# Decoder trunk on one core: TensorE's instructions chained in the order of emission

## The chip, the core and the metric

The kernel runs on one NeuronCore of one Trainium2 chip. A core has TensorE (PE; its weight loads are listed apart, as PEld), VectorE (DVE), ScalarE (ACT), GpSimd (POOL) and SyncE (SP, which issues the DMAs here). Each engine takes its own list of instructions in the order in which that list was written when the kernel was compiled, and waits on semaphores for what other engines must have done. The metric is the device time of one launch in microseconds. The kernel before takes 2995.44 us, the median of 3 runs (2991.24 to 2997.36).

## The reference

Two layers over 2048 prompt tokens and 8 sample tokens. Each layer projects the normed input, sends the columns through three mixers (mLSTM, Mamba-2 SSD, sliding-window attention), and projects back:

```python
def _layer(x, pos, conv_buf, ssm_h, C0, n0, m0, kc, vc, norm_w, w_in, ..., w_out):
    u = _rmsnorm(x, norm_w) @ w_in                      # 1024 -> 4880
    (aq, ak, av, ao, az, ai, af, bz, bxbc, bdt, cq, ck, cv, cz) = _split(u, IN_SIZES)
    ha, C1, n1, m1 = _mlstm(aq, ak, av, ai + a_ib, af + a_fb, C0, n0, m0)
    ya = _rmsnorm(ha, a_nw) * sigmoid(ao) * silu(az)
    xbc, conv1 = _causal_conv(bxbc, conv_buf, conv_w, conv_b)
    bx, bB, bC = _split(xbc, (B_WIDTH, B_GROUPS * B_STATE, B_GROUPS * B_STATE))
    yb, h1 = _ssd(bx, softplus(bdt + dt_bias), -exp(A_log), bB, bC, ssm_h)
    yb = _rmsnorm((yb + D_skip * bx) * silu(bz), b_nw)
    q, k = _rope(_rmsnorm(cq, qn_w), pos), _rope(_rmsnorm(ck, kn_w), pos)
    yc = _swa(q, k, cv, kc, vc, sinks) * silu(cz)       # window 128, softmax with sinks
    return x + concatenate([ya, yb, yc]) @ w_out, states   # 1536 -> 1024
```

Everything is float32; the states and the windows of keys and values are outputs too.

## The kernel before

**Tiling.** The prompt goes in blocks of 512 tokens: 4 blocks a layer, 8 in all. A block's input projection is done by groups of columns (`g0`, `qk`, `v`, `o`, `z`, `x0`, `x1`, `cq`, `cz`, `bz`), each of 8 chunks of 128 input features. The output projection of a block is two halves of 12 chunks, and it is put between groups `z` and `x0` of the next block. That makes 832 chunks.

**A chunk** (`multiply`, L500 to L542) is 12 matmuls, here called products: 4 banks (tokens or columns by 128) times 3 parts, because each float32 factor is cut into a high and a low part and three of the four part products are kept. In the first and the last chunk of a group all three parts of bank 0 come first, then those of bank 1, and so on. In the chunks between, the two products that need the high weight part come first for all four banks, then the third. L519 and L521 are the two forms of a product (weights moving or standing). In the first block of a layer, and in the output projection of its third, each chunk ends with two more matmuls for the sample tokens (L541, L542).

**PSUM.** A group accumulates in four banks (`pj`), which is all that the pool `pj` has, so the next group's bank t can only be written when the last group's bank t has been read out (evacuated). For `z`, `cz` and `bz` the read-out is a SiLU: a tanh on ACT (L561), then a product on DVE that reads the bank again (L562). The other groups are copied out by ACT, and the output projection by one DVE addition (L1291). The other four banks (`mx`) turn over among all the small work.

**The mixers** are Python generators, one step from `yield` to `yield`: mLSTM (`mix_a`, L837 to L873), SSD (`mix_b`, L951 to L995), attention (`pre_c`, `main_c`, L1108 to L1212), and more for gates, convolution, norms and sample tokens. In a chunk that isn't the last of its group, `pump` is called after every third product; at the end of every chunk it is called once. It goes through the streams in a fixed order and emits at most one step of each, when the stream's rate allows it and when a small model of the engines (`Clock`) holds the last step of the stream for finished and a bank for free. So in the emitted order, mixer work stands only after a multiple of three products: all PE instructions of a step are emitted in one piece.

**What sets the order.** The program is traced inside `tile.TileContext(nc, schedule_with_timeline_sim=True)`. At its end, the framework makes each engine's list: it plays the traced instructions through its own timing model and gives an engine, at each time of that model, the earliest emitted instruction that the model holds for ready. So the list of an engine can differ from the order of emission, and once made it is fixed. A few DMAs are pinned with `tc.keep_in_program_order`. The diff touches the end of `run` (L1832 to L1905).

Of the kernel before, what the change touches and what calls it, by code (L numbers as in the profile page):

```python
# [184 lines left out]
class Build:  # L185
# [1662 lines left out]
    def run(self):  # L1848
        nc = self.nc
        self.L = {0: self.layer_params(0)}  # L1850
        chunks = self.plan()
        PD, PS = 4, 2
        pre = self.dec_prep(0, None)
        self.con = con = self.consts()
        for i in range(PD):
            self.xraw(i)
            self.load_chunk(chunks[i])
            if i == 0:
                next(pre)
                next(con)  # L1860
        for i in range(PD, KD):
            self.xraw(i)
        for h in range(2):
            self.tokens(0, h, (12, 0)[h])
        for i in range(PS):
            self.xparts(i, self.L[0])
            self.split_chunk(chunks[i])
            self.flush()
        for _ in pre:
            pass  # L1870
        for i in range(PS, KD):
            self.xparts(i, self.L[0])
        grp = None
        for i, ch in enumerate(chunks):
            S = ch['S']
            if ch['pos'] == 0:
                self.before(ch)
                grp = self.banks(ch['dec'])
                if ch['g'] == 'out' and 'y' not in ch:
                    self.prep_y(ch)  # L1880
                    self.flush()
            if i + PD < len(chunks):
                self.load_chunk(chunks[i + PD])
            if i + PS < len(chunks):
                self.split_chunk(chunks[i + PS])
            if i + 1 < len(chunks) and chunks[i + 1]['g'] == 'out':
                nx = chunks[i + 1]
                self.drain(*({4: 'be', 0: 'a', 8: 'c'} if nx['S']['last'] else {0: 'c', 4: 'e'}).get(nx['k'], ''))
                self.prep_y(nx)
            if ch['g'] == 'out' and not S['last'] and ch['pos'] == (8 if ch['half'] == 0 else 5):  # L1890
                self.load_res(ch)
            if ch['g'] == 'out' and S['last'] and ('res', ch['half']) not in S and ch['k'] == (5 if ch['half'] else 0):
                self.load_res(ch)
            if ch['pos'] == ch['nk'] - 1:
                self.drain(*{'v': 'b', 'o': 'a', 'cq': 'ad', 'bz': 'v', 'x0': 'vs', 'x1': 'vs'}.get(ch['g'], ''))
            self.multiply(ch, grp)
            if ch['pos'] == ch['nk'] - 1:
                if ch['g'] == 'out':
                    self.evac_out_end(ch, grp[1])
                else:  # L1900
                    self.evac_end(ch['S'], ch['g'], grp[1])
            self.pump(ch['w'], BACKE if ch['pos'] >= ch['nk'] - EDGE else BACKO if ch['g'] == 'out' else BACK)
            self.lates()
            self.after(ch)
        self.flush()  # L1905


def build(nc):
# [27 lines left out]
```

## Time and profile before

| what | value |
| --- | --- |
| median of 3 runs | 2995.44 us |
| the profiled execution | 2994.12 us |
| its span, first to last instruction | 2992.3 us |
| PE busy | 2903.5 us, 97% |
| DVE, ACT, POOL busy | 1912.3, 1235.0, 920.3 us |
| DMA | 187 GB/s over the span |

A line of the timeline gives the start in us from the span's start, the length in us, engine, line of the kernel, operation, tile written and tiles read, shape, and how many like it follow without another of that engine between; in square brackets stands how long the engine had been idle before and what ended that. The length of a matmul is modelled and overlaps the next one, so the pace of PE is read from starts. A line of the waits gives the waiting engine with its tile and line, the releaser, the us in total, the number of waits and the longest. A line of the windows gives the stretch, its length, busy time and (x) count of PE, PEld, DVE, ACT and POOL, the granted TensorE clock (1.00 is 2.4 GHz, 0.50 is 1.2 GHz), the DMA share and GB/s.

### The profile page before, as it was taken

Reading aid. Unit: us, or ns where it says so; the run is one execution under the profiler, and the core shown is the slowest. Engines: PE = TensorE matmul, PEld = TensorE weight load, DVE = VectorE, ACT = ScalarE, POOL = GpSimd, SP = SyncE. Lnnn points to the kernel's source line nnn. Section 1 sums busy time; section 2 is a strip of 40 time slices with the busy share of each in tenths; the row PEclk is TensorE's granted clock in tenths of the full one; section 3 lists DMA queues with packets and bytes.
Section 4 is the critical chain, followed back from the end, with each engine's and each line's share of the span. In section 5 each row is a group of like instructions: output and inputs, shape, how many; then the busy total and the mean of one; then the engine's idle time right before and its main releaser. Section 6 shows DMA issues by size and latency. Waiting matters only on the chain.

```text
span 2992.3 us, 42253 instructions
## 1 busy us (share of the span) xinstructions
PE 2903.5 (97%) x14454; PEld 2373.4 (79%) x14454; DVE 1912.3 (64%) x4323; ACT 1235.0 (41%) x3219; POOL 920.3 (31%) x968
## 2 busy tenths in 40 slices
PE   8999999999999999999999999999999999999988
PEld 7787877788878888888788778887887778788876
DVE  6378567778476763477644686477755677645774
ACT  5343555235432453325544345432444225532344
POOL 5336325244131430116422552332421132200321
PEclk9999999999999999999999999999999999999999
DMA  8755558754575434655556745687545754355533
GB/s 279 241 197 168 174 184 284 248 170 141 164 247 189 151 117 143 199 171 182 184 187 215 240 159 183 205 274 232 161 156 177 244 174 160 131 163 165 177 112 124
DMA packets 245995, 558.82 MB, mean 187 GB/s; under 512 B 49308, under 2 KB 82236, under 8 KB 245732
## 3 DMA queue, kind: packets, MB, share of 16 engines
q1 hardware_dynamic: 245780, 556.12, 57.6%
q8 instruction: 114, 1.87, 0.3%
q14 instruction: 101, 0.83, 0.1%
HBM read 430.46 MB, written 127.87 MB: 187 GB/s over the span
## 4 chain that ended last, share of the span: by engine, by line
PE 71%; DVE 13%; DMA 8%; POOL 3%; ACT 2%; issue 2%; SPq 1%; POOLq 0%; DVEq 0%; ACTq 0%
PE pj L519 29%; PE pj L521 27%; DMA wr<-in_w_in 2%; PE mx L1203 2%; PE mx L1152 2%; PE mx L984 1%; DMA unit<-bcd 1%; DVE quad L659 1%; PE mx L542 1%; PE mx L541 1%; POOL hl L498 1%; ACT unit L1173 1%; PE mx L993 1%; PE mx L1252 1%; DMA unit<-us 1%
## 5 line engine op out<-in xcount | busy, mean ns | idle before, releaser
L521 PE MATMUL pj<-hl,xTh 128*128 128x512 f32 (+1 forms) x3072 | 945.4, 383 | 17.2 <-ACT hl L494 7.6
L519 PE MATMUL pj<-xTh,hl 128*128 128x512 f32 x2240 | 727.5, 402 | 4.8 <-ACT xTh L1259 2.9
L521 PEld LDWEIGHTS pj<-hl,xTh 128*128 128x128 f32 x3072 | 564.6, 189 | 129.0 <-DVE quad L562 8.3
L521 PE MATMUL pj<-hl,xTl 128*128 128x512 f32 (+1 forms) x1536 | 580.4, 381 | 0.0
L519 PE MATMUL pj<-parts,hl 128*128 128x512 f32 x2016 | 518.9, 404 | 15.1 <-DVE parts L1266 8.3
L519 PEld LDWEIGHTS pj<-xTh,hl 128*128 128x128 f32 x2240 | 421.5, 190 | 100.9 <-ACT xTh L1259 3.9
L519 PEld LDWEIGHTS pj<-parts,hl 128*128 128x128 f32 x2016 | 366.9, 189 | 96.1 <-DVE parts L1266 11.2
L519 PE MATMUL pj<-xTl,hl 128*128 128x512 f32 x1120 | 436.0, 398 | 1.9 <-DVE xTl L1266 1.9
L498 POOL TENSOR_TENSOR hl<-wr,hl 128x512 fp32r<-128x512 f32 (+1 forms) x232 | 318.9, 1380 | 356.3 <-ACT hl L494 311.2
L521 PEld LDWEIGHTS pj<-hl,xTl 128*128 128x128 f32 x1536 | 291.1, 189 | 52.5
L1195 POOL TENSOR_TENSOR parts<-parts,cst 128x512 fp32r<-128x512 f32 x120 | 158.6, 1339 | 409.0 <-ACT parts L1188 392.3
L519 PEld LDWEIGHTS pj<-xTl,hl 128*128 128x128 f32 x1120 | 211.2, 189 | 47.7 <-DVE xTl L1266 2.3
L1266 DVE SCALAR_TENSOR_TENSOR parts<-quad,lp,parts 128x512 fp32r<-128x512 f32 x168 | 143.0, 852 | 155.4 <-ACT quad L1263 62.4
L494 ACT ACTIVATE hl<-wr 128x512 fp32r<-128x512 f32 (+1 forms) x232 | 142.2, 615 | 234.2 <-PE mx L542 49.6
L1032 POOL TENSOR_TENSOR unit<-quad,rpqn 128x256 f32<-128x256 f32 x32 | 24.3, 759 | 441.6 <-PE mx L951 166.8
L1173 ACT ACTIVATE unit<-unit,c_m,c_sc 128x128 f32<-128x128 f32 x256 | 123.3, 483 | 69.3 <-DVE c_m L1164 68.8
L1259 ACT ACTIVATE parts<-quad,lp 128x512 fp32r<-128x512 f32 x112 | 80.4, 720 | 155.9 <-PE pj L519 141.1
L659 DVE SCALAR_TENSOR_TENSOR quad<-quad,lp,quad 128x512 f32<-128x512 f32 x192 | 141.8, 781 | 0.3
L1189 DVE TENSOR_TENSOR parts<-mx,parts 128x512 fp32r<-128x512 f32 x64 | 44.0, 687 | 90.2 <-ACT parts L1188 81.0
L384 POOL TENSOR_TENSOR quad<-quad 128x512 f32<-128x512 f32 x24 | 33.5, 1398 | 217.1 <-ACT quad L382 216.4
L1181 ACT ACTIVATE unit<-unit,c_m 128x128 f32<-128x128 f32 x256 | 81.3, 392 | 19.4 <-DVE c_m L1179 19.2
L541 PE MATMUL mx<-hl,samS 128*66 128x512 f32 (+1 forms) x208 | 83.4, 403 | 0.9 <-ACT hl L494 0.9
(409 smaller groups left out, 4551.3 us busy)
## 6 DMA issues: line engine op xcount, KB each, us to landing
hl<-kept SPq DMA_DIRECT2D x552, 512.0 KB
kept<-hl SPq DMA_DIRECT2D x184, 512.0 KB
wr<-in_w_in SPq DMA_DIRECT2D x168, 256.0 KB
hl<-kept SPq DMA_DIRECT2D x48, 272.0 KB
quad<-in_xT SPq DMA_DIRECT2D x40, 256.0 KB
quad<-in_x_prompt SPq DMA_DIRECT2D x16, 512.0 KB
wr<-in_w_out SPq DMA_DIRECT2D x32, 256.0 KB
x<-quad SPq DMA_DIRECT2D x32, 256.0 KB
```

The costliest lines, as they stand in the source:

```text
L494: nc.scalar.activation(h, r, AF.Copy)
L498: nc.gpsimd.tensor_tensor(lw, r, h.bitcast(F32), op=ALU.subtract)
L519: nc.tensor.matmul(ps[t], w[:, tt], a, start=st and first, stop=en and last)
L521: nc.tensor.matmul(ps[t][:, :N], a[:, tt], w[:, :N], start=st and first, stop=en and last)
L541: nc.tensor.matmul(pd[:66, :N], self.samS[:, k, :], hi[:, :N], start=st, stop=False)
L659: nc.vector.scalar_tensor_tensor(acc, u[:, j:j + 512], cw[:, j, c:c + 1], acc, op0=ALU.mult, op1=ALU.add)
L1152: nc.tensor.matmul(o, q, kz[:, a, s, 0:nk, :].rearrange("p n c -> p (n c)"), start=s == 0, stop=s == 1)
L1173: nc.scalar.activation(P(a, j), P(a, j), AF.Exp, bias=nm[:, j:j + 1], scale=head(sc, a, j), accum_out=den[:, j:j + 1])
L1181: nc.scalar.activation(P(a, j), P(a, j), AF.Copy, scale=den[:, j:j + 1])
L1195: nc.gpsimd.tensor_tensor(o.bitcast(F32R), p, self.triu.unsqueeze(1).to_broadcast([128, 4, 128]), op=ALU.mult)
L1259: nc.scalar.activation(yh.rearrange("p (t c) -> p t c", c=128), pt, AF.Copy, scale=L['ynw'][:, k:k + 1])
L1266: nc.vector.scalar_tensor_tensor(yl.rearrange("p (t c) -> p t c", c=128), blk, L['ynw'][:, k:k + 1], yh.bitcast(F32).rearrange("p (t c) -> ...
```

## The change

At the end of `run`, after everything has been emitted, `as_emitted('PE')` walks through all traced instructions and ties each one of TensorE to the TensorE instruction emitted just ahead of it. The tie is of class NoSync: it sets the place in the engine's list, and adds no semaphore and no wait. No instruction is added, removed or altered. The other engines and the DMA queue get no ties; their lists are still made by the framework's model, in which TensorE now goes through its instructions in this order.

```diff
@@ -1903,6 +1903,17 @@
             self.lates()
             self.after(ch)
         self.flush()
+        self.as_emitted('PE')
+
+    def as_emitted(self, engine):
+
+        last = None
+        for i in self.nc.cur_bb.bb.instructions:
+            if getattr(i.engine, 'name', str(i.engine)) == engine:
+                if last is not None:
+                    self.tc.add_manual_dep(i, last.name, mybir.DependencyInfo(
+                        mybir.DependencyClass.NoSync, mybir.DependencyReason.DATA), reason="as_emitted")
+                last = i
```

## Rows read from the trace of the kernel before

**Rows 1.** The page: span, and busy time of each engine.
```profile
span 2992.3 us, 42253 instructions
PE 2903.5 (97%) x14454; PEld 2373.4 (79%) x14454; DVE 1912.3 (64%) x4323; ACT 1235.0 (41%) x3219; POOL 920.3 (31%) x968
```

**Rows 2.** The waits of PE, three of the longest in total.
```profile
PE mx L984 <- DVE unit L979: 11.9, 6, 5.4
PE pj L519 <- DVE parts L1266: 8.3, 8, 2.4
...
PE pj L521 <- DVE quad L562: 6.4, 7, 2.8
```

**Rows 3.** Timeline of PE, 701.7 to 703.2 us: an SSD step between products.
```profile
701.90 0.39 PE L519 MATMUL pj<-xTl,hl 128*128 128x512 f32 x1
702.13 0.40 PE L519 MATMUL pj<-xTh,hl 128*128 128x512 f32 x1
702.37 0.60 PE L951 MATMUL mx<-ident,quad 128*128 128x128 f32 x4
702.72 0.48 PE L519 MATMUL pj<-xTl,hl 128*128 128x512 f32 x1
703.04 0.38 PE L956 MATMUL mx<-ident,quad 128*128 128x128 f32 x2
```

**Rows 4.** Timelines of ACT, POOL, PE, 682 to 691 us: inputs, readers.
```profile
685.64 1.27 ACT L1181 ACTIVATE unit<-unit,c_m 128x128 f32<-128x128 f32 x4
...
682.30 1.04 POOL L989 TENSOR_TENSOR unit<-unit,X 128x512 f32<-128x512 f32 x1 [5.47 <-PE mx L984]
...
689.44 1.02 PE L993 MATMUL mx<-unit,unit 128*128 128x256 f32 x4
...
690.77 0.60 PE L1186 MATMUL mx<-ident,unit 128*128 128x128 f32 x4
```

**Rows 5.** Timelines of DVE and PE behind cz, third block, 991 to 1000.
```profile
993.00 4.62 DVE L443 SCALAR_TENSOR_TENSOR quad<-quad,lp,keys 128x512 f32<-128x512 f32 x4
997.54 2.47 DVE L562 SCALAR_TENSOR_TENSOR quad<-wP,pj 128x512 f32<-128x512 f32 x4
...
991.40 0.39 PE L519 MATMUL pj<-xTh,hl 128*128 128x512 f32 x1
...
993.23 1.10 PE L965 MATMUL mx<-hst,quad 128*128 128x256 f32 x4 [0.68 <-DVE unit L953]
...
998.27 0.50 PE L521 MATMUL pj<-hl,xTh 128*128 128x512 f32 x1 [2.83 <-DVE quad L562]
```

**Rows 6.** Timeline behind group bz, fourth block, 1394 to 1398.4 us.
```profile
1394.10 0.63 PE L1152 MATMUL mx<-kz,parts 128*128 128x256 f32 x4
...
1396.13 0.29 PE L521 MATMUL pj<-hl,xTh 128*128 128x272 f32 x1
...
1397.66 0.68 DVE L562 SCALAR_TENSOR_TENSOR quad<-wP,pj 128x512 f32<-128x512 f32 x1
```

**Rows 7.** Timelines of PE and DVE behind z, fourth block, 1160 to 1165.
```profile
1160.29 0.39 PE L521 MATMUL pj<-hl,xTh 128*128 128x512 f32 x1
...
1163.81 2.49 PE L519 MATMUL pj<-parts,hl 128*128 128x512 f32 x10
...
1164.31 0.68 DVE L562 SCALAR_TENSOR_TENSOR wP<-wP,pj 128x512 f32<-128x512 f32 x1
```

**Rows 8.** Windows before and behind the wait that ends at 998.27 us.
```profile
985.00:995.00 10.00, 9.32 (x52) 7.41 (x51) 9.31 (x13) 4.66 (x10) 9.28 (x16) 1.00 0.64 203
...
999.30:1002.60 3.30, 3.30 (x9) 2.63 (x8) 3.24 (x7) 0.58 (x1) 1.28 (x1) 0.50 0.26 80
```

**Rows 9.** Timeline of PE, 1734 to 1742 us: a wait inside a chunk.
```profile
1734.50 0.40 PE L519 MATMUL pj<-xTl,hl 128*128 128x512 f32 x1
1738.67 2.46 PE L984 MATMUL mx<-unit,unit 128*128 128x64 f32 x16 [3.77 <-DVE unit L979]
...
1741.64 1.97 PE L519 MATMUL pj<-xTh,hl 128*128 128x512 f32 x4
```

## The prediction

> **What bounds the kernel now.** I read the page first: TensorE is busy for 2903.5 us of a span of 2992.3 us [rows 1]. The reader is to see that nothing else comes near it, and that 88.8 us of idle time is all that any order of the same instructions could win. Next came the waits of TensorE: the longest in total is 11.9 us, for one kind of SSD matmul, and the others are under 9 us each [rows 2]. Then the timeline of TensorE at places where mixer work stands among products, and at the borders between two groups of columns, for there the list of an engine can differ from the order of emission. An engine takes its list as it stands. So the question is not whether TensorE can go around a wait, but which of two fixed lists leaves it waiting longer.
>
> **What the change moves.** It adds and removes no instruction and no semaphore; TensorE's work stays at 2903.5 us. What moves is where mixer steps stand among the products. Emission puts a step in one piece, after a multiple of three products. The trace shows something else: the four transposes L951 and the two L956 are one step, yet a product stands between them, and the step starts two products behind a hand-over point [rows 3]. Of the 32 such steps 16 are split, by 11 products on average over all 32; the pace of products is 0.23 us [rows 3], so that is 2.5 us. Of the 64 turns of the probabilities (L1186) 30 begin at a place where no step can be emitted, and chance alone would put a third of the moved ones on a lawful place, so some 45 of 64 have moved. The order thus changes in much of the program, mostly by a few products.
>
> **First term: borders between groups.** A new group needs the four banks of the old one. Behind `z`, `cz` and `bz` these are read out by ACT and then DVE, which is slow; there are 24 such borders. Three of them:
> - Behind `cz` the last product starts at 991.40, and DVE reads out the banks only from 997.54 on, since four operations L443 for the next block lie ahead of it in DVE's list. TensorE did mixer steps meanwhile, sat idle for 2.83 us, and went on at 998.27 [rows 5]. In emitted order one hand-over follows the last product, some 0.9 us of steps, and then bank 0 is needed: idle from 992.5 to 998.2, 5.7 us, against the 3.5 us of before (the 2.83 and another 0.68). Cost 2.2 us.
> - Behind `bz` the fill runs from 1394.10 to 1396.13, sample matmuls of later chunks in part, and products of the next two chunks for the free banks follow while bank 3 is read out until 1398.34 [rows 6]. In emitted order the second chunk can't start before the fourth bank of the first: nine products of 0.13 us (1396.13 on, 272 columns) and nine sample matmuls as short drop out of the stretch. Cost 2.3 us.
> - Behind `z` the last product starts at 1160.29, the products go on at 1163.81, and bank 3 comes free at 1164.99 [rows 7]. In order, nine products (2.1 us) and at most one hand-over lie between, 4.5 us in all. Cost about 2 us.
> Work that filled a border isn't lost, but it must then be done where TensorE had no hole. 24 borders at 2.0 us make 48 us. Bounds: nothing, if the read-outs come earlier because the fill no longer feeds DVE and ACT; and 84 us, if each border loses the 3.5 us that TensorE filled or slept behind `cz`.
>
> **Second term: steps that come before their inputs.** A step that was moved back by 2.5 us loses that much margin. The margins are wide: the normalised probabilities were finished at 686.91 (685.64 and 1.27) and their turn began at 690.77, 3.86 us later; a POOL product ended at 683.34 and its matmul began at 689.44 [rows 4]. Over the 64 pairs of the first kind the median is 4.6 us and a tenth is under 0.8; over the 32 of the second 4.3 and 0.7. With 18 steps that hold TensorE work for each 128 tokens, 32 times, there are 576 of them. About a fifth has less than 2.5 us; at 0.5 us each that is 58 us, and since a wait in one stream gives time to the two others I take half, 30 us. Below, nothing; above, a quarter of the steps at 1.2 us, 170 us.
>
> **Third term: the clock.** After the wait that ended at 998.27 the granted clock was 0.50 (1.2 GHz) from 999.3 to 1002.6, against 1.00 before; nine matmuls ran in these 3.30 us, where 14 fit at 0.23 us [rows 3, 8]. That lost 1.2 us. If ten borders get a wait of that length that they haven't now: 12 us; I take 10. Bounds 0 and 40 us. The Trainium skill, "TensorE: Matmul & The Clock Gate", section "HAM oscillation — how this bites in real kernels", warns of idle gaps of TensorE for the same reason and so speaks against this change. By this rule the sum holds the third term; without it the sum is 10 us lower. The trace agrees with the rule at this place.
>
> **Fourth term: waits that go.** Some steps stand earlier now than they were emitted, and TensorE waits there with products behind. Not all of that goes: L984 waits 3.77 us until 1738.67 with products of its own chunk behind it [rows 9], but it stands eight products into the chunk, one or two from a lawful place, so it would wait in either list. Of the listed waits, those on mixer lines come to some 40 us, and I let 25 us go. Bounds 0 and 45 us.
>
> **The sum.** The profiled execution took 2994.1 us, 1.3 us less than the median of the runs; that is nothing beside the terms. 2994 + 48 + 30 + 10 - 25 = 3057 us. ACT, DVE, POOL and the DMA queue keep their work, and the model that makes their lists sees TensorE wait more, so those lists change too; I have no row to cost that, and it is in the bounds of the first two terms. What covers the first term now is the fill of the borders, and with that gone each late read-out is bare.
>
> **The rivals.**
> - *Faster: the fill is what makes the read-outs late.* Steps pulled into a border hand ACT and DVE work that stands in front of the read-out or beside it. Without them the banks come free sooner, the first and third term vanish, steps meet their inputs as the emitting model meant it, and about half of the 88.8 us idle time goes: 2994 - 45 = 2950 us. For it: the margins of rows 4, and the pace of emission, which asks for finished steps before it emits the next. Against: behind `cz` what stood ahead of the read-out was the norm of the next block, which TensorE's order doesn't govern [rows 5]. It decides if the read-out behind `z`, `cz`, `bz` ends within nine products, 2.1 us, of each bank's last product.
> - *Much slower: margins are used up.* If the moves are of the size of the splits in most steps and the inputs move along with them, the second term is at its upper end: 2994 + 48 + 120 + 15 - 15 = 3160 us or more. For it: half of the SSD steps are split now. Against: margins of about 4 us.
> - *No change: gains and losses meet, or the order matters little.* If TensorE passed by a waiting matmul, the list would not matter and the time stay at 2994 us. Against: in rows 9 products whose chunk had already begun stood behind the waiting matmul, and none was run for 3.77 us.
>
> **How the numbers follow.** The forecast case (borders and some steps) has 0.50, much slower 0.18, faster 0.24, no change 0.08. About 0.2% or 6 us is what a measurement can tell from no change. So slower 0.68, same 0.08, faster 0.24. For the forecast case alone, the bounds of the first term and the middle of the others give 3010 to 3110 us. The range leaves out a tenth at each end: below it half of the faster case, above it half of the much slower one: 2955 to 3180 us.
>
> **What would show it.** Right: TensorE busy as before, its idle time up by 50 us or more, most of it on L519 and L521 released by DVE L562 or by ACT; no product of a second chunk before the fourth bank of the first; no split step; more stretches at clock 0.50. Second term: waits on L984, L1186, L1203, L993 that add up to some 30 us more. Wrong: idle time below 88.8 us, with L562 close behind the last product, or the waits mostly on `mx` banks rather than on inputs, which I have not costed apart.

## The result and the profile after

The chained kernel takes 3110.05 us (median of 4 runs, 3106.74 to 3115.2), the kernel before beside it 2994.41 us: 1.0388 times as long, 95% interval 1.0371 to 1.0404. Slower, as forecast, but by 116 us where 62 were forecast. The profiled execution has a span of 3110.4 us, 118.1 more than before.

The page after; the first two lines answer to [rows 1]:

```profile
span 3110.4 us, 42210 instructions
...
PE 2955.3 (95%) x14454; PEld 2400.2 (77%) x14454; DVE 1928.9 (62%) x4323; ACT 1245.2 (40%) x3219; POOL 930.9 (30%) x968
```

With the same 14454 matmuls, TensorE is busy 51.8 us longer, and its idle time goes from 88.8 to 155.1 us, 66.3 more. The prediction had TensorE's busy time unchanged; this part of the loss, not quite half, lies outside the waits altogether. Most of it is the clock: the matmuls that ran at a granted clock of 0.50 fill 128.8 us, against 41.6 before. What such work loses is read from the pace of the products. Here is the kernel before in the stretch at 0.50 of [rows 8]:

```profile
1000.58 0.63 PE L521 MATMUL pj<-hl,xTl 128*128 128x512 f32 x1
1001.00 1.05 PE L521 MATMUL pj<-hl,xTh 128*128 128x512 f32 x2
1001.86 0.63 PE L521 MATMUL pj<-hl,xTl 128*128 128x512 f32 x1
```

Three products start in 1.28 us, 0.43 us apart, against 0.23 at 1.00 [rows 3]. At these paces the 87.2 us more at half clock cost 40 us (an estimate that goes by the products alone). That the clock is lower doesn't hang on one profile: its mean was 0.976 to 0.978 in the four runs, and 0.987 to 0.992 in the runs of the kernel before.

The waits of TensorE after (tile and line, releaser, us in total, number, longest); the counterparts of [rows 2] are the L984 line and the first line:

```profile
PE pj L521 <- DVE quad L562: 15.9, 15, 2.9
PE mx L1332 <- DVE unit L1329: 15.6, 1, 15.6
PE mx L961 <- DVE rtB L792: 14.5, 5, 3.7
PE mx L984 <- DVE unit L979: 13.2, 8, 4.1
PE pj L519 <- DVE wP L562: 8.6, 11, 1.8
...
PE pj L519 <- DVE parts L1266: 6.2, 4, 1.7
PE mx L842 <- DVE rtA L792: 5.2, 6, 1.3
PE mx L956 <- DVE hst L995: 5.0, 5, 1.1
```

The reader is to see two kinds: products behind a SiLU read-out (both L562 lines, 24.5 us), and steps whose operand comes late from DVE. L961, with 14.5 us the longest of these inside the program, waits 0.5 us in all in the kernel before. L1332 is the program's start: the sample's transposes were emitted ahead of the first product, so TensorE now begins with them:

```profile
15.62 1.02 PE L1332 MATMUL mx<-ident,unit 8*128 8x8 f32 x8 [15.62 <-DVE unit L1329]
16.57 0.80 PE L521 MATMUL pj<-hl,xTh 128*128 128x512 f32 x1
```

Before, the first product began at 6.42 us and L1332 followed at 17.30. That is 9.2 us which the prediction did not see.

To tell the terms apart I put the idle time ahead of each TensorE instruction down to a product (L519, L521) or to a step (everything else), and to a place: *border* is the last chunk of a group and the first two of the next, *interior* the rest, found by counting twelve products a chunk (a step counts where it ran, one that stands between two chunks with the later of them). The wait at the program's start is left out. The last column is TensorE's busy time in stretches with a granted clock of 0.50. Times are medians of the runs; the other columns come from one profile each, in us.

| kernel | time | border idle: products, steps | interior idle: products, steps | at half clock: border, interior |
| --- | --- | --- | --- | --- |
| before | 2994 | 19.8, 30.5 | 12.8, 13.7 | 19.2, 22.4 |
| chained (after) | 3110 | 47.1, 23.5 | 2.7, 62.1 | 72.0, 56.8 |
| e3 steps only | 3025 | 23.9, 40.8 | 10.2, 18.4 | 41.4, 17.7 |
| e4 products only | 3023 | 28.3, 34.1 | 8.6, 15.6 | 47.5, 22.7 |
| e5 borders free | 3072 | 20.2, 6.5 | 7.1, 90.9 | 17.8, 90.5 |
| e6 interiors free | 3131 | 54.1, 79.3 | 7.9, 10.2 | 149.2, 15.7 |
| e9 step not ahead of product | 3074 | 63.4, 31.8 | 8.9, 15.7 | 60.0, 33.4 |
| e10 product not ahead of step | 3076 | 11.0, 27.3 | 5.3, 67.3 | 33.0, 62.3 |
| e1 all four engines chained | 3181 | 47.7, 35.5 | 8.9, 81.2 | 98.6, 70.5 |
| e2 TensorE and DVE chained | 3143 | 40.6, 23.5 | 7.0, 88.9 | 57.7, 69.3 |
| e11 chained, wait filled | 3118 | 47.2, 21.7 | 2.2, 60.9 | 67.4, 61.2 |
| e7 chained, later emission | 3298 | 57.9, 142.5 | 1.6, 48.9 | 197.8, 57.4 |
| e12 not chained, later emission | 3114 | 32.2, 95.6 | 8.0, 21.1 | 87.5, 17.9 |

From the first two rows: +27.3 us for products at borders, +48.4 for steps in the interior, -17.1 for the two kinds of wait that shrank, +9.2 at the start, -1.4 at the end, +40 for the clock, and some 12 of busy time left over: 118 us. Of these 12 about 7 are an estimate from the way in which busy time is counted: a matmul's modelled length is 0.39 us, of which only 0.23 count where the next one follows at once, and there are 44 more waits of over 0.15 us.

### The profile page after: what moved, and what is told of

Read it like the earlier page. It is cut to its first block, busy times and chain, and to the rows that moved or that the text cites. A ratio compares the mean times of both kernels' runs of the same rounds, so it can differ in the third digit from the quotient of the medians.

```text
span 3110.4 us, 42210 instructions
## 1 busy us (share of the span) xinstructions
PE 2955.3 (95%) x14454; PEld 2400.2 (77%) x14454; DVE 1928.9 (62%) x4323; ACT 1245.2 (40%) x3219; POOL 930.9 (30%) x968
## 4 chain that ended last, share of the span: by engine, by line
PE 65%; DVE 18%; DMA 7%; issue 4%; ACT 3%; POOL 2%; SPq 0%; POOLq 0%; ACTq 0%; DVEq 0%
PE pj L519 28%; PE pj L521 23%; PE mx L1152 2%; PE mx L1203 1%; DVE quad L443 1%; PE mx L984 1%; DVE quad L659 1%; PE mx L542 1%; PE mx L541 1%; POOL hl L498 1%; DMA quad<-x 1%; DMA unit<-qd 1%; PE mx L857 1%; DMA unit<-bcd 1%; PE mx L1186 1%
## 5 line engine op out<-in xcount | busy, mean ns | idle before, releaser
L521 PE MATMUL pj<-hl,xTh 128*128 128x512 f32 (+1 forms) x3072 | 971.0, 386 | 18.4 <-DVE quad L562 15.9
L519 PE MATMUL pj<-xTh,hl 128*128 128x512 f32 x2240 | 753.7, 407 | 4.0 <-ACT kvg L592 3.9
L521 PEld LDWEIGHTS pj<-hl,xTh 128*128 128x128 f32 x3072 | 571.7, 191 | 139.3 <-DVE quad L562 23.4
L521 PE MATMUL pj<-hl,xTl 128*128 128x512 f32 (+1 forms) x1536 | 582.2, 382 | 0.0
L519 PE MATMUL pj<-parts,hl 128*128 128x512 f32 x2016 | 525.5, 406 | 26.6 <-DVE wP L562 8.6
L519 PEld LDWEIGHTS pj<-xTh,hl 128*128 128x128 f32 x2240 | 425.7, 192 | 99.6 <-ACT kvg L592 4.4
L519 PEld LDWEIGHTS pj<-parts,hl 128*128 128x128 f32 x2016 | 370.7, 190 | 112.4 <-DVE wP L562 14.2
L519 PE MATMUL pj<-xTl,hl 128*128 128x512 f32 x1120 | 440.2, 400 | 0.8 <-DVE xTl L1266 0.8
L521 PEld LDWEIGHTS pj<-hl,xTl 128*128 128x128 f32 x1536 | 294.4, 192 | 52.3
L1195 POOL TENSOR_TENSOR parts<-parts,cst 128x512 fp32r<-128x512 f32 x120 | 167.4, 1412 | 411.6 <-ACT parts L1188 400.8
L494 ACT ACTIVATE hl<-wr 128x512 fp32r<-128x512 f32 (+1 forms) x232 | 142.5, 615 | 277.4 <-PE mx L542 96.4
L519 PEld LDWEIGHTS pj<-xTl,hl 128*128 128x128 f32 x1120 | 213.6, 191 | 45.9 <-DVE xTl L1266 1.2
L1211 DVE TENSOR_TENSOR unit<-unit,mx 64x512 f32<-64x512 f32 x64 | 43.8, 684 | 109.0 <-ACT unit L1210 108.3
L653 ACT ACTIVATE quad<-quad 128x512 f32<-128x512 f32 x64 | 40.5, 634 | 119.4 <-DVE quad L659 118.9
L1181 ACT ACTIVATE unit<-unit,c_m 128x128 f32<-128x128 f32 x256 | 82.0, 394 | 11.0 <-DVE c_m L1179 11.0
```

Source lines behind the costliest of these rows:

```text
L494: nc.scalar.activation(h, r, AF.Copy)
L519: nc.tensor.matmul(ps[t], w[:, tt], a, start=st and first, stop=en and last)
L521: nc.tensor.matmul(ps[t][:, :N], a[:, tt], w[:, :N], start=st and first, stop=en and last)
L1181: nc.scalar.activation(P(a, j), P(a, j), AF.Copy, scale=den[:, j:j + 1])
L1195: nc.gpsimd.tensor_tensor(o.bitcast(F32R), p, self.triu.unsqueeze(1).to_broadcast([128, 4, 128]), op=ALU.mult)
L1211: TT(o, o, pO[a][rr], op=ALU.add)
```

## One step, before and after

The step that waits at L961 shows what the order of before had done. Here is the kernel before, TensorE, at the second SSD step of the second block:

```profile
641.49 0.27 PE L788 MATMUL mx<-identb,LR 128*120 128x128 bf16 x2
641.60 0.61 PE L951 MATMUL mx<-ident,quad 128*128 128x128 f32 x4
...
646.23 0.38 PE L956 MATMUL mx<-ident,quad 128*128 128x128 f32 x2
646.37 1.18 PE L521 MATMUL pj<-hl,xTh 128*128 128x512 f32 x4
647.38 0.61 PE L961 MATMUL mx<-rtB,ltB 120*128 120x512 bf16 x2
```

and DVE in that time:

```profile
641.99 1.22 DVE L792 TENSOR_TENSOR rtB<-mx,cst 120x1024 bf16<-120x1024 bf16 x1
...
644.32 2.73 DVE L443 SCALAR_TENSOR_TENSOR quad<-quad,lp,keys 128x512 f32<-128x512 f32 x4
```

L788 gives DVE what it needs to make `rtB` (L792). The step is split between L951 and L956 by 4.3 us of products; `rtB` is ready at 643.21, L961 reads it at 647.38. This is the kind of split that [rows 3] show. The same step after, TensorE (no split any more), and then DVE:

```profile
662.75 0.27 PE L788 MATMUL mx<-identb,LR 128*120 128x128 bf16 x2
662.86 0.61 PE L951 MATMUL mx<-ident,quad 128*128 128x128 f32 x4
664.32 0.44 PE L956 MATMUL mx<-ident,quad 128*128 128x128 f32 x2 [0.85 <-DVE hst L995]
664.51 0.48 PE L519 MATMUL pj<-xTl,hl 128*128 128x512 f32 x1
...
665.76 0.40 PE L519 MATMUL pj<-xTh,hl 128*128 128x512 f32 x1
669.35 0.61 PE L961 MATMUL mx<-rtB,ltB 120*128 120x512 bf16 x2 [3.19 <-DVE rtB L792]
```

```profile
665.60 2.42 DVE L443 SCALAR_TENSOR_TENSOR quad<-quad,lp,keys 128x512 f32<-128x512 f32 x2
667.95 0.21 DVE L791 COPY ltB<-mx 120x128 bf16<-120x128 bf16 x1
668.08 1.21 DVE L792 TENSOR_TENSOR rtB<-mx,cst 120x1024 bf16<-120x1024 bf16 x1
```

Six products after the step comes its reader, while DVE is still at L443 of the next block; L961 waits 3.19 us and every product stands behind it. Over all 32 such pairs the median time from the end of L792 to L961 falls from 4.0 to 1.2 us, and those under 0.5 us go from 2 to 11. Two things changed, and the four waits of over 3 us for `rtB` tell them apart: the way from L788 to L961 (without the wait) went from 3.6 to 5.6 us down to 3.1 to 3.4, and `rtB` was finished 6.3 to 7.0 us after L788 where it had been 1.4 to 4.1. Over the four that is some 5 us of shorter way and some 16 us of later operand: DVE's list, which was made anew, did more here than the lost split. Of the two pairs that the prediction had measured instead [rows 4], one went the other way, from L1181 to L1186 a median of 4.6 to 7.8 us, and the other, from L989 to L993, went from 4.3 to 3.8.

## The experiments

**Is it the other engines' lists?** In the trace above DVE's list, made by the framework, has L443 of a later block ahead of the L792 that TensorE's list wants. If two orders that don't fit are the trouble, chaining the others too should mend it.

```diff
-        self.as_emitted('PE')
+        for e in ('PE', 'DVE', 'Activation', 'Pool'):
+            self.as_emitted(e)
```

> The changed kernel with VectorE's, ScalarE's and GpSimd's lists tied in the emitted order as well, each instruction to the one emitted ahead of it on its engine. Theory L (the changed kernel loses because TensorE stands in one order and the other engines' lists in another, so that the operand of a step, like rtB at L961, is made behind later work): the 41 us that mixer and sample steps gained in idle time go, and the time is about 3,060 us or less, the L961 waits of 3 us are no longer in the trace. Theory M (each step now stands in one place and has no margin there, whatever the order of the others): the time stays at 3,110 us or rises, since the other engines now also wait at the head of their lists.

The second run has `('PE', 'DVE')` in that place.

> The changed kernel with VectorE's list tied in the emitted order too, ScalarE and GpSimd free. Theory L: most of the gain of tying all four comes with VectorE alone, since the late operand at L961 (rtB, L792) stands behind L443 of a later block on VectorE: 3,060 to 3,085 us. Theory M: 3,110 us or more.

Measured: 3181.0 us with all four (ratio 1.0622, 1.0596 to 1.0647) and 3143.37 with two (1.0494, 1.0474 to 1.0515). The waits of TensorE with all four chained:

```profile
PE mx L412 <- DVE keys L409: 26.0, 7, 4.8
PE pj L521 <- DVE quad L562: 21.2, 14, 2.7
...
PE mx L715 <- DVE CS L710: 12.6, 4, 3.6
```

L961 has left the list of long waits, and L412 and L715 are new at its head. So the theory holds for one wait and falls for the time: with DVE in emitted order another operand is late. What the mixture of two orders costs in the chained kernel is not told apart by this, since chaining DVE brings waits of its own; shown is only that lists that fit one another are no cure.

**Which order costs: that of the steps, of the products, or between them?** Products (L519, L521) are noted by name when they are emitted; in one run only the others are tied to each other, in the next only the products.

```diff
-            if getattr(i.engine, 'name', str(i.engine)) == engine:
+            if getattr(i.engine, 'name', str(i.engine)) == engine and i.name not in self.products:
```

> Only TensorE's instructions of the mixer and of the sample are tied to one another; the products (L519, L521) are left to the framework, which may put them ahead of a step or behind it. If the steps' order among themselves costs (a step that is late holds the next step), the time is above 3,050 us. If the loss comes from where the steps stand among the products (no margin, borders), the time is within 15 us of the 2,994 us of the kernel before.

> Only the products (L519, L521) are tied to one another; the steps are free to move among them. The products' own order hardly differs from the emitted one in the kernel before, so that every theory that lays the loss on the steps' places expects 2,994 us within 10 us here; a time near 3,110 us would lay it on the products, that is on the weights and banks that they take in turn.

Measured: 3025.37 us (1.0104, 1.0084 to 1.0124) and 3023.39 (1.0096, 1.0076 to 1.0115). Each kind alone costs 27 to 29 us. Both expectations missed: the first time lies between its two cases (within 15 us of 2,994, or above 3,050), and the products' own order was thought to be as emitted, within 10 us. If the two costs add up, which no run shows, they make 55 of the 116 us, and the rest belongs to the order of steps against products.

**Borders or interiors?** What is emitted in the last chunk of a group and in the first two of the next is noted, and left out of the chain, or alone kept in it.

```diff
+            if ch['pos'] < 2 or ch['pos'] == ch['nk'] - 1:
+                self.border |= {x.name for x in nc.cur_bb.bb.instructions[mark:]}
...
-                if last is not None:
+                if last is not None and i.name not in self.border:
...
-                last = i
+                last = i if i.name not in self.border else None
```

> TensorE stays chained inside the groups, but what is emitted in the last chunk of a group and in the first two of the next is left to the framework. The prediction's first term (borders cost 48 us) expects 3,110 - 48, about 3,060 us. The trace after shows 25 us more idle time of products in the first chunk of a group, with half-clock stretches behind it: by that, 3,070 to 3,085 us. If the places inside the groups make the loss, the time stays within 15 us of 3,110 us.

> The reverse: chained only in the last chunk of a group and the first two of the next, free between. If borders cost 48 us, as predicted, 2,994 + 48, about 3,042 us; by the idle time in the trace after, 3,020 to 3,035 us; if only the places inside the groups cost, within 10 us of 2,994 us. If the two parts add up, the losses of this run and the gains of the one with free borders agree.

Measured: 3072.17 us (1.0256, 1.0236 to 1.0275) with borders free, 3130.85 (1.0456, 1.0438 to 1.0475) with interiors free. The first is where the trace after put it. The second missed: chaining the borders alone costs 137 us, more than chaining everything. The table shows why: the waits are found where the chain is. With interiors free the interior is no worse than before (18.1 us idle; before 26.5), and the borders hold 133.4 us against 50.3. L984 alone waits 36.3 us in that run, in 9 waits, against 13.2 in the chained kernel; behind `cz` of the second to fourth block it waits 5.7 to 5.8 us each time. With borders free they hold 26.7 us, and the interiors 98.0 against 64.8 in the chained kernel. A wait that is lifted at one place is partly paid at the next; the two parts don't add up.

**In which direction did the free order help?** Products chained to products, steps to steps, and of the ties between the kinds only one direction:

```diff
-                if last is not None:
...
-                last = i
+                kind = i.name in self.products
+                for k in ((True,) if kind else (True, False)):
+                    if k in last:
...
+                last[kind] = i.name
```

In the second run the loop is over `((True, False) if kind else (False,))`.

> Products are chained to one another and steps to one another, as in the two runs with one kind tied (3,025 and 3,023 us), and of the ties between the two kinds only one direction is kept: a step may not stand ahead of the product emitted before it, but products may stand ahead of a step. If the loss is that products stand behind steps whose operands are late, it goes: 3,020 to 3,050 us. If it is that steps can't be pulled forward into a hole, such as a border, it stays: near 3,110 us.

> The other direction: a product may not stand ahead of the step emitted before it, but a step may stand ahead of products. If the loss is that products stand behind steps whose operands are late, it stays: 3,090 us or more. If it is that steps can't fill holes, it goes: 3,020 to 3,050 us. Between the two runs the lost 116 us should be found once; if each direction alone keeps more than half of it, the two losses overlap.

Measured: 3074.14 us (1.0269, 1.0253 to 1.0285) and 3075.81 (1.0270, 1.0255 to 1.0285): each freedom wins back some 35 us, and neither gives the time that its own theory had asked for. Each run keeps 80 us, more than half, but that is no sign of an overlap, as the expectation would have it: both runs also keep the chains within the kinds. If those cost 55 us together, each direction adds some 25 us and the two together 61. The two losses sit at different places. Waits of TensorE where products may go ahead of a step:

```profile
PE pj L521 <- DVE quad L562: 16.4, 18, 2.3
PE mx L984 <- DVE unit L979: 12.9, 6, 3.7
```

and where a step may go ahead of products:

```profile
PE mx L984 <- DVE unit L979: 19.6, 10, 5.0
...
PE mx L961 <- DVE rtB L792: 10.9, 5, 4.3
...
PE pj L521 <- DVE quad L562: 4.7, 5, 1.5
```

In the first the steps' idle time in the interior is back at 15.7 us (before 13.7, chained 62.1): it came with products that must stand behind a late step. But the other engines' lists are made anew in each run, and the operands are less late as well: where L961 waited over 3 us in blocks two to four and six of the chained kernel, `rtB` is finished 1.4 to 5.3 us after L788 in this run, against 6.3 to 7.0. What of the gain is the passing and what the earlier operand is not told apart. In the second that of products at borders is 11.0 us (before 19.8, chained 47.1): it came from steps that can't be drawn into the hole while the banks are read out. Behind `z`, `cz` and `bz` some 21 step instructions stand between the last product and the first one for bank 3, against 11 in the chained kernel, and bank 3 is read out no sooner (4.2 us behind the start of the last product, against 3.7). The L562 line is 16.4 us in the one and 4.7 in the other; L961 waits 10.9 us in the second and 2.4 in the first.

**Would steps emitted later have margin?** The chained kernel, and the kernel before, with one constant changed, so that the emitting model holds a step back until what it needs has been ready for 1.5 us by its reckoning:

```diff
-CAP, SLACK, RAW, BACK, BACKO, BACKE, EDGE = 2.5, 0.0, 125.0, 2900.0, 3300.0, 1500.0, 2
+CAP, SLACK, RAW, BACK, BACKO, BACKE, EDGE = 2.5, -1500.0, 125.0, 2900.0, 3300.0, 1500.0, 2
```

> The changed kernel, all of TensorE chained, but the emitting model lets a step go only if what it needs has been ready for 1.5 us by its reckoning (SLACK -1500 in place of 0), so that steps are emitted some six products later. If the loss inside the groups comes from steps that stand there without margin, the idle time ahead of mixer and sample steps (85.5 us in the changed kernel) falls to some 60 us, and the half-clock stretches with it: 3,060 to 3,085 us. If margins aren't what is missing, or if later steps pile up where a group's streams must be finished, 3,110 us or more.

> The kernel before, without any ties, with the same later emission as in the margin run (SLACK -1500), which took 3,298 us with ties. If the framework's own order makes up for a bad emission, 2,994 to 3,030 us; if the later emission itself fills the ends of the groups with steps that no order can take from there, 3,100 us or more.

Measured: 3297.86 us chained (1.1010, 1.0990 to 1.1031), 3113.5 unchained (1.0402, 1.0384 to 1.0419). Interior step waits do fall, from 62.1 to 48.9 us, but those at borders rise from 23.5 to 142.5: the steps held back are emitted together where a group's streams must be finished. Unchained, the framework takes back 184 of these 304 us, though 95.6 us of step waits at borders remain. So more margin, given everywhere at once, is no cure; and the chain costs 184 us on this emission against 116 on the original one.

**Does idle time bring the clock down?** Three float32 matmuls (six records) ahead of L961, overwritten by L961 itself, in four of the blocks.

```diff
-            pE = [self.mx() for _ in range(2)]
+            pE = [self.mx() for _ in range(2)]; (c == 1 and S['n'] in (0, 1, 3, 5)) and self.fill(pE[0], xbc[4][:, 0:512])
...
+    def fill(self, out, x):
+        self.clock.run()
+        t = self.clock.t['PE']
+        for _ in range(3):
+            self.nc.tensor.matmul(out, self.ident, x, start=True, stop=True)
+        self.clock.run()
+        self.clock.t['PE'] = t
```

In the first run they stood, against its expectation, at the stream's first step (`c == 0`), a step ahead of the wait, and the emitting model counted them.

> The changed kernel with three float32 matmuls put in front of the L961 that waits 2.5 to 3.7 us for rtB in four of the blocks (near 277, 669, 1420 and 2210 us); what they write is overwritten by L961 itself. They run in the wait. If idle time of TensorE is what brings the granted clock down to 0.50 behind these four waits (some 16 us of half-clock time there), the clock stays at 1.00 there, and the time falls by up to 8 us, to about 3,102 us. If the clock falls for another reason, the stretches at 0.50 stay and the time is 3,110 us.

> As the run that filled the wait ahead of L961, but at the second step of the SSD stream in the four blocks, where the waits of 2.5 to 3.7 us in the changed kernel are (277, 669, 1420, 2210 us), and with the emitting model kept from counting the three float32 matmuls, so that the emitted order stays as it was. In the run before they stood at the first step, 17 to 30 us earlier, where nothing waits, and cost their own time (4 x 2.6 us; measured 9 us). If idle time brings the clock down there, the granted clock behind L961 is 1.00 in place of 0.50 at these four places and the time falls by up to 8 us to about 3,102; if it falls for another reason, 0.50 stays and the time is within 3 us of 3,110.

Measured: 3119.32 us (1.0418, 1.0402 to 1.0434) in the first, which tells only what four times 2.6 us of added work cost, 9 us; and 3118.47 (1.0420, 1.0403 to 1.0436) in the second, where 3,102 or 3,110 had been expected. The time refutes the 8 us gain; the trace shows where it went. Timeline of TensorE in the second run, second block:

```profile
665.20 2.74 PE L1922 MATMUL mx<-quad,ident 128*128 128x512 f32 x6
668.43 0.59 PE L961 MATMUL mx<-rtB,ltB 120*128 120x512 bf16 x2 [0.49 <-DVE rtB L792]
...
672.55 0.69 PE L1108 MATMUL mx<-ident,unit 128*128 128x128 f32 x2 [2.67 <-DVE unit L953]
```

Windows of that run, behind L961 and behind the new wait (stretch, length, busy time of five engines, granted clock, DMA share, GB/s):

```profile
668.40:671.00 2.60, 1.46 (x6) 0.85 (x5) 2.60 (x2) 1.08 (x2) 2.44 (x3) 1.00 0.09 28
672.50:676.00 3.50, 3.44 (x14) 3.16 (x15) 2.49 (x6) 1.80 (x4) 3.50 (x8) 0.55 0.16 53
```

The same place in the chained kernel, behind its 3.19 us wait:

```profile
669.40:672.40 3.00, 3.00 (x13) 2.44 (x13) 3.00 (x3) 1.56 (x4) 2.92 (x3) 0.60 0.09 25
```

With the wait filled (0.49 us of it is left here, 1.45 and 1.65 in the fourth and sixth block), the clock behind L961 stays at 1.00 (2.4 GHz) where it was 0.60, a mean of the two levels. It is the same in the fourth and sixth block: 1.00 behind L961 against 0.61 and 0.50. In all three a new wait of about 2.67 us follows one step on, at L1108, for DVE's L953, and a stretch at 0.50 begins beside that wait or just behind it (672.3, 1426.6 and 2215.1 us). The first block tells nothing: its wait of 2.5 us was for L953 and not for `rtB`, and in the new run the clock was at 0.50 from 272.9 to 276.3 us already, ahead of the fill. So where a low stretch comes it follows the wait, shown at three places of this one run and at the three new waits. Over the whole program nothing was won: the matmuls at half clock fill 128.6 us (128.8 without the fill), idle time fell by 3.3 us, and the fills themselves are 11 us of work. What the clock's whole share would do without waits is not shown.

No version came out that beats the kernel before: every chain that was tried costs time.

## Why the prediction was right in sign and short in size

**First term (borders, 48 us): too large, for the read-outs came sooner.** Idle time of products at borders rose by 27.3 us. In the first chunk behind `z`, `cz` and `bz`, the 24 borders of the sum, it rose from 9.5 to 24.7, so 0.6 us a border and not 2.0. With the waits of steps in the same chunk, 13.6 us before and none after, the idle time there hardly changed, 23.1 to 24.7. The fill did go, but bank 3 was read out on average 3.7 us behind the start of the last product, where it had been 5.6. Behind the first half of the output projection, which the prediction left out, idle time of products rose from 3.5 to 11.7. The three examples, one by one:

- `cz` [rows 5]: 5.7 us of idle time were forecast, 0.86 came. In TensorE and DVE after:

```profile
1053.87 0.40 PE L519 MATMUL pj<-xTh,hl 128*128 128x512 f32 x1
1055.13 0.50 PE L521 MATMUL pj<-hl,xTh 128*128 128x512 f32 x1 [0.86 <-DVE quad L562]
```

```profile
1053.66 0.69 DVE L1120 TENSOR_TENSOR parts<-mx,parts 64x512 fp32r<-64x512 f32 x1
1054.38 2.48 DVE L562 SCALAR_TENSOR_TENSOR quad<-wP,pj 128x512 f32<-128x512 f32 x4
```

  The four L443 that stood ahead of the read-out before are done by 1046.72 now. The step that failed is "TensorE's order doesn't govern" what stands ahead in DVE's list: the framework made that list anew. Here the read-out came sooner, as the rival "faster" had it, but not for its reason (what stood ahead was no work of the fill), and not within the 2.1 us that it needed: bank 3 is free 3.0 us behind the start of the last product.
- `bz` [rows 6]: 2.3 us forecast. TensorE after:

```profile
1460.77 0.40 PE L521 MATMUL pj<-hl,xTh 128*128 128x512 f32 x1
1463.06 0.40 PE L521 MATMUL pj<-hl,xTh 128*128 128x272 f32 x1 [1.89 <-DVE quad L562]
...
1465.46 0.59 PE L521 MATMUL pj<-hl,xTh 128*128 128x272 f32 x1 [1.16 <-DVE quad L562]
```

  Two waits, 3.05 us, with no sample matmul or second chunk between them, as forecast.
- `z` [rows 7]: about 2 us forecast, 0.84 measured in two waits, for banks 2 and 3:

```profile
1222.48 0.97 PE L519 MATMUL pj<-parts,hl 128*128 128x512 f32 x3 [0.55 <-DVE wP L562]
1223.74 0.96 PE L519 MATMUL pj<-parts,hl 128*128 128x512 f32 x3 [0.29 <-DVE wP L562]
```

That the lost fill is the cause of the idle time that is left is shown by e10, where steps may be drawn forward again and that of products at borders falls to 11.0 us, with bank 3 read out no sooner.

**Second term (steps before their inputs, 30 us): mis-sized, and its sample misled.** Steps in the interior wait 48.4 us more; e9, which lets products pass late steps, takes 46 of it back. The forecast spread a loss of 2.5 us of margin over pairs like those of [rows 4], of which one kind grew and the other lost about half a us, and halved the result because "a wait in one stream gives time to the two others". The step that failed is "A step that was moved back by 2.5 us loses that much margin", with the input left in its place: of the 48.4 us, 28.5 came at L961, L956 and L842, whose margins were never read, and at the long L961 waits the operand came 2.9 to 5.1 us later while the way to its reader shrank by 0.3 to 2.5.

**Third term (clock, 10 us): the largest miss, some 40 us by the traces.** The working took one border with one stretch at 0.50 [rows 8] and ten borders. There were 10 stretches before and there are 27 now (the last of each holds no matmul), 24 of them at or close behind a wait of over 1 us, and most of the new ones have nothing to do with `cz`. Behind the `bz` waits above, the clock is low for 10.2 us:

```profile
1465.00:1475.20 10.20, 9.74 (x44) 9.75 (x45) 4.27 (x6) 3.01 (x11) 6.33 (x8) 0.52 0.36 108
```

At the paces above some 4.4 us of the 9.74 busy us are lost (an estimate): more than the 3.05 us of waiting. The term had too few waits, since steps make waits too. But not each wait has its price. Of the waits of over 2 us inside the program 17 of 19 have a stretch at 0.50 beside or close behind them (8 of 12 before), of those between 1 and 2 us 10 of 30 (3 of 15). A wait of 3.28 us at L961, at 1043.8 us, has none, and the same one, of 3.05 us, has one in the run that filled other waits. The upper bound of 40 us is just reached. The price of one stretch was a little small too: at 0.43 us a product the 3.30 us of [rows 8] hold 7.7 products and not nine, a loss of 1.5 us. And the 88.8 us are not all that an order could win, since 41.6 us of work ran at half clock before. The Trainium skill's section "HAM oscillation — how this bites in real kernels" ("TensorE: Matmul & The Clock Gate") speaks of the same effect; the trace bears it out at four times the size that the sum gave it.

**Fourth term (waits that go, 25 us): about right.** Steps at borders wait 7.0 us less and products in the interior 10.1 less, 17 us. L984 still waits (13.2 us in 8 waits, [rows 2, 9] before), as the prediction expected of its example: 4.0 us until 1811.0, where it was 3.77.

**Not in the sum:** 9.2 us at the start, which can be read from the order of emission alone (`dec_prep` is run to its end before the loop); e5, which leaves this part free, begins at 7.1 us.

**The signs that it named.** The idle time rose by more than the 50 us, no step is split any more, and there are more stretches at 0.50, as it said. Two signs failed. Most of the new idle time was to be on products released by L562 or by ACT: L562 rose from 7.1 to 24.5 us, but ACT's part fell from 18.0 to 6.1. And L984, L1186, L1203 and L993 were to wait some 30 us more: they went from 23.3 to 27.2.

So the total landed within the range, and the idle time came near its forecast (66.3 us against 48 + 30 - 25 = 53) by luck: the first term was too large and the second too small by about as much. The clock made most of the shortfall. Of the rivals, "much slower" was nearer in time than in mechanism: its margins were not all used up (the median from L792 to L961 is still 1.2 us). "No change" was wrong: in e9 and e10 freeing one direction alone moves the time by 35 us.

**What stays open.** Why chaining the borders alone costs more than chaining everything, beyond that waits shift; why the operand of L1108 is late where L961 is early; why some waits bring the clock down and others as long don't; and what idle time the framework's model expects at the places where it keeps L443 ahead. None of these was tried.

## What to carry over

Instructions of a step that a list-making program has spread among other work may look like disorder; look at what the gap gives to the engine that makes the next operand before tying them together, and read the margin of the reader behind each gap, not of a pair that is easy to find. Cost an order by both directions: what can no longer be drawn forward into a hole, and what can no longer pass a late instruction; chaining one kind of work alone cost a quarter of the whole here. Count also on the other engines: their lists were made anew with the ties, and operands and read-outs moved too, at the four long waits of L961 by more than the steps. And give new TensorE waits, all together, a price for the clock, which here was some 60% of the added idle time itself.

## What was not expected of the hardware

The clock's share: 66.3 us more idle time came with some 40 us lost to work at half clock. At single places the second is larger than the first (3.05 us of waits at 1463 to 1465 us, then 10.2 us at 0.52). It isn't the length of a wait alone that tells: one of 3.28 us left the clock at 1.00, and one of 1.18 us (L993 in the kernel before, at 292.6 us) stood beside a stretch at 0.50. And a fill of 2.74 us in an otherwise idle TensorE kept the granted clock at 1.00 in three of three places.
